# The tail of a two-layer decoder trunk: order of VectorE's scalings and last statistics, and low weight parts made by ScalarE and adding transfers

## The chip, the cores and the metric

The kernel runs on one core of a Trainium2 chip. The metric is the device time of one execution in microseconds; the median of three runs counts. A profile is one further execution, recorded by the hardware profiler, with a span from its first to its last instruction. The engines are TensorE (PE, its weight loads PEld), VectorE (DVE), ScalarE (ACT), GpSimd (POOL) and SyncE (SP), which issues nearly all DMAs.

## The reference

Two decoder layers over 256 positions of width 2048, all in float32. Layer 0 mixes by a gated short convolution, layer 1 by multi-head latent attention; each is followed by a squared-ReLU MLP of hidden width 8192, and every sub-layer ends in a layer norm of the scaled residual and the result. What matters here is the end:

```python
def sq_relu_mlp(x, w1, w2):
    return jnp.square(jax.nn.relu(x @ w1)) @ w2

h = layer_norm(ALPHA * h + mix, ln_g[layer, 0], ln_b[layer, 0])
h = layer_norm(ALPHA * h + sq_relu_mlp(h, mlp_w1[layer], mlp_w2[layer]),
               ln_g[layer, 1], ln_b[layer, 1])
```

## The kernel before, in words

**Two parts of a number.** TensorE multiplies in a rounded float32 form. To keep the precision, each operand is split in a high part (rounded) and a low part (what the rounding lost), and a product is the sum of three: high by high, high by low, low by high. A weight of 128 x 1024 numbers (a "half", 512 KB) is loaded into a buffer called raw (`load_raw`, issued on SP); `split` (L137 to L140) has ScalarE cast it into hi (L139) and VectorE subtract hi from raw into lo (L140). There are 7 raw buffers and 9 buffers of each part. A raw buffer comes free when its last reader, as a rule the subtraction on L140, is done.

**Slots.** An MLP (`mlp`) walks through a list of slots. A slot of the up-projection multiplies two w1 halves with the activations into ps_u (32 matmuls), which `evacuate` sums with a ScalarE copy (L401) and a VectorE addition (L402); beside it most slots multiply one "fast pair" of w2 weights, which go through a scheme of seven products in place of eight and need extra VectorE work: a difference of the two loads (L172), two more (L177, L179) and four splits, six steps in all (`prepare`, `to_step`). Each slot also prepares what the next one needs: its w1 halves (`singles`) and its pair (`pairs`). After each slot `order.keep()` ties the instructions of TensorE, VectorE and ScalarE to the order in which they were written. DMAs on SP and GpSimd are not tied; SP takes its own in one order, and a load waits there until a raw buffer is free. What comes after the slots is not tied on any engine: there the order is the one that the scheduler of the framework chose when the program was built.

**The end of the last MLP.** The last slots are (7, 7), with the last w1 halves and the third of four pairs, and (8, 0), with the last pair alone. Of w2's last quarter two column blocks are left over, n = 0 and n = 1, which are multiplied plainly: eight halves, called p0 to p7 here, p0 to p3 for n = 0 and p4 to p7 for n = 1. p0 to p4 are the singles of slot (8, 0); `take`, which looks ahead, prepares p5 to p7. `down_late` multiplies them for both token halves (t = 0: the first 128 positions, t = 1: the rest), t outside and n inside as written, so p0 serves twice. Between the first two blocks, `between` has VectorE finish the sums of the fast products (`fold_last`, L681) and take the statistics of the blocks 2 and 3.

**The last norm** (`to_out`). `finished` (L1204) takes statistics of each of the four blocks (L1205). After the last one of a token half, VectorE aggregates them (L1211) and computes the inverse deviation (rr, L431). For t = 0 it centres each block (L1219), scales it (L1222), and SP stores it (L1197). For t = 1, ScalarE makes diagonal matrices of means (L1232) and deviations (L1239), TensorE adds their products with gamma and beta (gbt) to three of the blocks (L1235) and one (L1240), VectorE scales three blocks (L1222) and ScalarE the last (L1244). The whole of gbt is loaded on SP (L1190), into the room that the activations of the up-projection leave.

**Adding transfers.** The first fold of the fast products (`fold`, g = 0, L668) is made by GpSimd DMAs which add one SBUF block to another.

Of the kernel before, what the change touches and what calls it, by code (L numbers as in the profile page):

```python
# [10 lines left out]
F32 = mybir.dt.float32  # L11
F32R = mybir.dt.float32r
AF = mybir.ActivationFunctionType
ALU = mybir.AluOpType
# [42 lines left out]
def trunk(ctx: ExitStack, tc: tile.TileContext, xT, vecs, lead, w_first, w_in, w_out, w_kv, w_q, w_uk, w_uv,  # L57
# [79 lines left out]
    def split(hi, lo, src):  # L137

        nc.scalar.copy(hi, src)  # L139
        return nc.vector.tensor_tensor(lo, src, hi.bitcast(F32), ALU.subtract)  # L140

    def tiled(w):
        return w.rearrange("p (b c) -> p b c", c=P)
# [9 lines left out]
    def prepare(i):  # L153

        if len(stream[i]) == 1:
            raw = loaded.pop(i) if i in loaded else load_raw(i, stream[i][0])
            hi, lo = ready[i] = parts(i)
            split(hi, lo, tiled(raw))
            yield
            return  # L160
        r1, r2 = (load_raw(f"{i}_{j}", src) for j, src in enumerate(stream[i]))
        t = raws.tile([P, 1024], F32, tag="raw", name=f"raw{i}_t")
        out = []

        def finished(r, name):
            hi, lo = parts(name)
            split(hi, lo, tiled(r))
            out.append((hi, lo))

        b22, (b21, b12) = r1[:, BW:], (r2[:, :BW], r2[:, BW:])  # L170
        two = "p (a c) -> p a c"
        nc.vector.tensor_tensor(t.rearrange(two, a=2), b12.unsqueeze(1).to_broadcast([P, 2, BW]),  # L172
                                r1.rearrange(two, a=2), ALU.subtract)
        yield
        finished(r1, f"{i}_1")
        yield
        nc.vector.tensor_tensor(b12, b22, t[:, :BW], ALU.subtract)  # L177
        t4 = r1[:, :BW]
        nc.vector.tensor_tensor(t4, b21, b12, ALU.subtract)  # L179
        yield  # L180
        finished(t, f"{i}_t")
        yield
        finished(r2, f"{i}_2")
        yield
        f = state["fast"].tile([P, 2, BW], F32R, tag="t4", name=f"t4_{i}", bufs=2)
        split(f[:, 0, :], f[:, 1, :], t4)
        b1, t13, b2 = ([[v.rearrange("p b c -> p (b c)")[:, o:o + BW] for v in w] for o in (0, BW)] for w in out)
        ready[i] = {"11": b1[0], "22": b1[1], "21": b2[0], "T2": b2[1], "T1": t13[0], "T3": t13[1],
                    "T4": [f[:, 0, :], f[:, 1, :]]}
        yield  # L190
# [2 lines left out]

        return 1 if len(stream[i]) == 1 else 6

    begun, loaded = {}, {}

    def step(i):

# [421 lines left out]
    def mlp(idx, ln, blocks, fast, begin=None, extra=None, last=False):  # L621
# [192 lines left out]
        for s, (q, m, pair, own) in enumerate(slots):  # L814
            lone = pair is None
            following = slots[s + 1][3] if s + 1 < len(slots) else []
            pairs = [i for i in following if size(i) > 1]
            far = slots[s + 2][3][-1:] if s + 2 < len(slots) and not pairs and lone else []
            far = [i for i in far if size(i) > 1]
            end = following[-1] + 1 if pairs else far[0] if far else own[-1] + 6  # L820
            singles = [i for i in range(state["next"], end) if i not in own and size(i) == 1 and i not in begun]
            for i in singles:
                loaded[i] = load_raw(i, stream[i][0])
            if q == FAST[0] and m == SHIFT:
                sums = act.tile([P, 4, 2, BW], F32, tag="xres", name=f"sums{idx}")
                for o, _, _ in FACTORS:
                    resume(o, 1)
            if q < NQ:
                w = take(2, 0)
                at = "6" if lone and (m - SHIFT) % 2 else "unit"  # L830
                un = psum("ps_u", bank[at])
                mm_run([(w, un)], xhl, 0, NC, NC, turned=TURNED if TURN(q, m) else None)

            def to_step(n):

                for i in pairs:
                    while i not in begun or begun[i][1] < n:
                        step(i)

            def evacuate():  # L840

                if q == NQ:
                    return
                if m % 2 == 0:
                    rows[m // 2] = fast.tile([P, 8 * P], F32, tag="fp", name="fp")
                u = rows[m // 2]
                whole(un, u[:, (m % 2) * T:(m % 2 + 1) * T])
                if m == QC - 1:
                    nc.vector.scalar_tensor_tensor(u[:, T:2 * T], u[:, T:2 * T], 0.0, u[:, T:2 * T], ALU.max, ALU.mult)
                    forms(u)  # L850
                    due.extend((m // 2, at) for at in columns(m))

            crowded = len(moves) > 0
            ends = q == NQ - 1 and m == QC - 1
            if q == NQ and last:
                last_sum(0, 0, bank["unit"])
            to_step(1)
            if not singles or m == 0 or q == NQ:
                split_due()
            for i in singles:  # L860
                step(i)
                move(1)
                drain()
                split_due()
            if crowded:
                evacuate()
                move(len(moves))
            if q == NQ - 1 and m == SHIFT and not last:
                fold_some(4)
            if q == NQ - 1 and m == 2:  # L870
                fold_some(8)
            if far:
                for i in far:
                    for _ in range(2):
                        step(i)
            if q == NQ - 1 and m == QC - 2 and not last:
                fold_some(4)
            hi_first = pairs and not crowded and q < NQ
            to_step(1 if hi_first else 2)
            if pair:  # L880
                products_of(*pair)
            if not crowded:
                if hi_first:
                    to_step(2)
                evacuate()
            move(1)
            to_step(3)
            if ends:
                split_due()
            to_step(4)  # L890
            move(1)
            to_step(5)
            move(1)
            to_step(6)
            move(1)
            if q < NQ:
                if m % 2 and m < QC - 1 or m == QC - 2:
                    u = rows[m // 2]
                    at = u[:, :T] if m == QC - 2 else u[:, :2 * T]
                    for function in (AF.Relu, AF.Square):  # L900
                        nc.scalar.activation(at, at, function)
                    if m % 2:
                        forms(u)
                    due.extend((m // 2, at) for at in columns(m))
                if extra and q == FAST[0] and m < NB:
                    for t in range(2):
                        extra(block, m, t, spare[1 + (2 * m + t) % 3])
                if begin and q == FAST[0] and m < 4 and m % 2 == 0:
                    nc.gpsimd.dma_start(parked[:, 4 * m:4 * m + 8, :], held_x[0][:, 4 * m:4 * m + 8, :])
                for i in far:  # L910
                    for _ in range(2):
                        step(i)
            order.keep()
# [273 lines left out]
    def to_out(block, finals, h, fold_last):  # L1187
# [8 lines left out]
        def store(t, i):  # L1196
            nc.sync.dma_start(out[t * P:(t + 1) * P, i * BW:(i + 1) * BW], block(i, t))  # L1197

        def scratch(i):
            return raws.tile([P, 1024], F32, tag="raw", name=f"u{i}")[:, :BW]  # L1200

        order = (2, 3, 0, 1)

        def finished(n, t, ps):  # L1204
            nc.vector.bn_stats(out=stats[:, t, n, :], in_=ps)  # L1205
            if n != order[-1]:
                if t == 1:
                    nc.vector.tensor_tensor(ps, ps, gbt[:, n, :BW], ALU.mult)
# [10 lines left out]
                nc.vector.scalar_tensor_tensor(us[i], finals[i, t], mv[:, 0:1], gbt[:, i, :BW], ALU.subtract, ALU.mult)  # L1219

            def scaled(i, x, other, op=ALU.add):
                nc.vector.scalar_tensor_tensor(block(i, t), x, r, other, ALU.mult, op)  # L1222
                store(t, i)

            if t == 0:
                rsqrt(r, ve)
                for i in order:
                    centred(i)
                    scaled(i, us[i], gbt[:, i, BW:])
                return  # L1230
            means = scratch("means")[:, :P]
            nc.scalar.activation(means, negative, AF.Copy, scale=mv[:, 0:1])  # L1232
            one = order[0]
# [4 lines left out]
            devs = scratch("devs")[:, :P]  # L1238
            nc.scalar.activation(devs, id_t, AF.Copy, scale=ve)  # L1239
            nc.tensor.matmul(finals[one, t], devs, gbt[:, one, BW:], start=False, stop=True, skip_group_check=True)  # L1240
            scaled(n, us[n], gbt[:, n, BW:])
            for i in order[1:-1]:
                scaled(i, finals[i, t], gbt[:, i, BW:])
            nc.scalar.activation(block(one, t), finals[one, t], AF.Copy, scale=r)  # L1244
            store(t, one)

# [105 lines left out]
```

## Time and profile before

| | |
|---|---|
| median of three runs | 1996.42 us (1995.43 to 1997.84) |
| profiled execution | 1996.9 us |
| its span | 1995.1 us |
| TensorE, VectorE, ScalarE, GpSimd busy | 99%, 88%, 64%, 1% |
| TensorE's mean granted clock | 0.998 |
| DMA moved | 394.19 MB, 198 GB/s on average |

A row of a timeline gives the start and the length in us, the engine, the line, the operation and what it writes and reads, and in brackets how long the engine was idle before and what ended that. Instructions of one kind in a row stand merged in one row (x5); they overlap at their edges, so that their sum of lengths is over their distance. A row of the windows gives, for each stretch, its length and the busy time and instructions of PE, PEld, DVE, ACT and POOL, then the granted clock of TensorE, the busy share of the DMA engines and GB/s. The chain of waits is followed back from the last instruction.

### The profile page before, as it was taken

What the parts mean: (1) busy time and instruction counts of PE and PEld (TensorE: products, weight loads), DVE (VectorE), ACT (ScalarE), POOL (GpSimd) and SP (SyncE); (2) the same over time, 40 slices, a digit from 0 to 9 for tenths busy, and PEclk for the clock granted to TensorE, in tenths of its full rate; (3) what the DMA queues carried; (4) which work ended last, traced back from release to release, by engine and by line L of the source; (5) the groups of instructions that cost most, each with busy time, mean ns of one, the idle gap of its engine ahead of it and who ended that gap; (6) DMA issues with size and microseconds to landing.
All of it is one profiled execution on the core that took longest, in us unless ns stands there. A gap on an engine that the chain in (4) does not pass through costs nothing.

```text
span 1995.1 us, 29544 instructions
## 1 busy us (share of the span) xinstructions
PE 1984.8 (99%) x11050; PEld 1730.0 (87%) x11050; DVE 1755.7 (88%) x2546; ACT 1278.5 (64%) x1872; POOL 19.7 (1%) x43
## 2 busy tenths in 40 slices
PE   9999999999999999999999999999999999999998
PEld 8888888988888888888889998898888888888886
DVE  8667667786999999999898988777899999999998
ACT  6444445585767767677656655557576776767763
POOL 0000000000000000000100000000000000000010
PEclk9999999999999999999999999999999999999999
DMA  9666666574566665566865544665366666666674
GB/s 342 212 190 188 190 190 190 178 236 131 200 203 203 210 202 192 206 204 211 270 245 159 181 137 131 187 191 180 127 211 201 201 197 203 211 203 202 198 231 158
DMA packets 110016, 394.19 MB, mean 198 GB/s; under 512 B 12208, under 2 KB 12976, under 8 KB 109360
## 3 DMA queue, kind: packets, MB, share of 16 engines
q1 hardware_dynamic: 106560, 383.79, 59.5%
q0 software_dynamic: 3168, 8.39, 1.7%
q8 instruction: 86, 1.41, 0.3%
q14 instruction: 58, 0.48, 0.1%
q10 hardware_dynamic: 144, 0.13, 0.0%
HBM read 383.87 MB, written 4.19 MB: 195 GB/s over the span
## 4 chain that ended last, share of the span: by engine, by line
PE 94%; DVE 3%; ACT 1%; DMA 1%; issue 1%; DVEq 0%; ACTq 0%
PE ps_u L256 20%; PE ps_l L256 13%; PE ps_u L260 10%; PE ps L343 7%; PE ps L344 7%; PE ps L341 7%; PE ps_l L260 7%; PE ps_d L344 2%; PE ps_d L343 2%; PE ps_d L341 2%; PE ps_w L290 1%; PE ps_w L288 1%; PE ps_w L289 1%; DVE lo L140 1%; PE ps_g L288 1%; PE ps_g L290 1%
## 5 line engine op out<-in xcount | busy, mean ns | idle before, releaser
L140 DVE TENSOR_TENSOR lo<-raw,hi 128x1024 fp32r<-128x1024 f32 x710 | 852.1, 1220 | 115.8 <-ACT hi L139 47.4
L139 ACT CAST hi<-raw 128x1024 fp32r<-128x1024 f32 x710 | 729.2, 1051 | 336.1 <-DVE raw L177 136.9
L256 PE MATMUL ps_u<-xhl,hi 128*128 128x512 f32 x1792 | 621.0, 393 | 0.4 <-DVE fp L402 0.3
L260 PE MATMUL ps_u<-xhl,lo 128*128 128x256 f32 x1792 | 485.4, 280 | 0.0
L256 PEld LDWEIGHTS ps_u<-xhl,hi 128*128 128x128 f32 x1792 | 329.1, 187 | 67.8 <-DVE fp L402 1.6
L260 PEld LDWEIGHTS ps_u<-xhl,lo 128*128 128x128 f32 x1792 | 338.0, 189 | 12.7
L256 PE MATMUL ps_l<-xhl_a,hi 128*128 128x512 f32 x704 | 244.1, 393 | 0.0
L260 PE MATMUL ps_l<-xhl_a,lo 128*128 128x256 f32 x704 | 195.4, 279 | 0.0
L256 PEld LDWEIGHTS ps_l<-xhl_a,hi 128*128 128x128 f32 x704 | 132.1, 188 | 29.9
L260 PEld LDWEIGHTS ps_l<-xhl_a,lo 128*128 128x128 f32 x704 | 131.9, 188 | 0.2
L172 DVE TENSOR_TENSOR raw_t<-raw,raw 128x1024 f32<-128x1024 f32 x100 | 121.8, 1218 | 1.6 <-DMA raw<-in_w2f_dram 1.6
L140 DVE TENSOR_TENSOR lo_t<-raw_t,hi_t 128x1024 fp32r<-128x1024 f32 x100 | 121.9, 1219 | 0.0
L401 ACT COPY t<-ps_u 128x256 f32<-128x256 f32 x112 | 41.5, 370 | 108.7 <-PE ps_u L260 108.4
L139 ACT CAST hi_t<-raw_t 128x1024 fp32r<-128x1024 f32 x100 | 105.3, 1053 | 0.1
L256 PE MATMUL ps_l<-z,hi 128*128 128x512 f32 x240 | 82.4, 391 | 0.0
L290 PE MATMUL ps_w<-xd,hi 128*128 128x258 f32 x256 | 72.7, 284 | 0.0
L288 PE MATMUL ps_w<-xd,hi 128*128 128x258 f32 x256 | 72.3, 282 | 0.0
L179 DVE TENSOR_TENSOR raw<-raw 128x512 f32<-128x512 f32 x100 | 69.2, 692 | 3.5
L289 PE MATMUL ps_w<-xd,lo 128*128 128x258 f32 x256 | 72.2, 282 | 0.0
L256 PE MATMUL ps_l<-oT,hi 128*128 128x512 f32 x208 | 71.3, 391 | 0.0
L402 DVE TENSOR_TENSOR fp<-ps_u,t 128x256 f32<-128x256 f32 x112 | 46.9, 418 | 27.7 <-ACT t L401 27.5
L140 DVE TENSOR_TENSOR t<-raw,t 128x512 fp32r<-128x512 f32 x100 | 68.5, 685 | 2.1 <-ACT t L139 1.6
(365 smaller groups left out, 3896.7 us busy)
## 6 DMA issues: line engine op xcount, KB each, us to landing
raw<-in_w_dram SPq DMA_DIRECT2D x312, 512.0 KB, 4.2
raw<-in_w2f_dram SPq DMA_DIRECT2D x200, 512.0 KB, 4.2
raw<-in_w_in_dram SPq DMA_DIRECT2D x88, 512.0 KB, 4.3
raw<-in_w_out_dram SPq DMA_DIRECT2D x32, 512.0 KB, 3.6
raw<-in_w_o_dram SPq DMA_DIRECT2D x32, 512.0 KB, 4.2
raw<-in_w_kv_dram SPq DMA_DIRECT2D x10, 512.0 KB, 5.0
raw<-in_w_q_dram SPq DMA_DIRECT2D x8, 512.0 KB, 4.0
raw<-in_w_uk_dram SPq DMA_DIRECT2D x8, 512.0 KB, 4.5
```

Source lines behind the costliest of these rows:

```text
L139: nc.scalar.copy(hi, src)
L140: return nc.vector.tensor_tensor(lo, src, hi.bitcast(F32), ALU.subtract)
L172: nc.vector.tensor_tensor(t.rearrange(two, a=2), b12.unsqueeze(1).to_broadcast([P, 2, BW]), r1.rearrange(two, a=2), ALU.subtract)
L179: nc.vector.tensor_tensor(t4, b21, b12, ALU.subtract)
L256: nc.tensor.matmul(ps, w[blk // 8][0][:, blk % 8, :], x, start=first, stop=False)
L260: nc.tensor.matmul(ps[:, :T], w[blk // 8][1][:, blk % 8, :], x[:, :T], start=False, stop=last)
L288: nc.tensor.matmul(ps[:, :W], hi, x[k][:, :W], start=k == 0, stop=False)
L289: nc.tensor.matmul(ps[:, :W], lo, x[k][:, :W], start=False, stop=False)
L290: nc.tensor.matmul(ps[:, :W], hi, x[k][:, W:], start=False, stop=k == NC - 1)
L341: nc.tensor.matmul(ps, x[0], w[0], start=first, stop=False, skip_group_check=onto)
L343: nc.tensor.matmul(ps[:, at], x[0], w[1][:, at], start=False, stop=False, skip_group_check=onto)
L344: nc.tensor.matmul(ps, x[1], w[0], start=False, stop=last, skip_group_check=onto)
```

## The change

It has two parts.

The first ties VectorE's order in the end. The last statistics (n = 1, t = 1) come behind the third scaling of t = 0. The fourth scaling of t = 0 (n = 1), with its store, is made only in the call for t = 1, behind the scaling of its block n, and the other two scalings of t = 1 follow in that order.

The second makes the low parts of p0 and p1 without VectorE. Both are loaded at the beginning of slot (7, 7), before the loads of the last pair. In that slot ScalarE casts hi, and then writes the negated hi into lo; a DMA of GpSimd adds the weight to it, which it reads from DRAM once more. p0's part stands ahead of `evacuate`, p1's behind it. In slot (8, 0) only p2 to p4 are left as singles.

```diff
@@ prepare
+            if i in summed_up:
+                nc.scalar.copy(hi, tiled(raw))
+                nc.scalar.activation(lo, hi.bitcast(F32), AF.Copy, scale=-1.0)
+                nc.gpsimd.dma_start(lo, tiled(stream[i][0]), accum_op=ALU.add)
+            else:
+                split(hi, lo, tiled(raw))
@@ mlp, the loop over slots
-            for i in singles:
+            ends = q == NQ - 1 and m == QC - 1
+            plain = [slots[-1][3][-1] + 1 + i for i in range(2)] if ends and last else []
+            summed_up.update(plain)
+            for i in singles + plain:
                 loaded[i] = load_raw(i, stream[i][0])
...
+                for i in plain[:1]:
+                    step(i)
                 evacuate()
+                for i in plain[1:]:
+                    step(i)
@@ to_out
+        def after(made, other):
+            tc.add_manual_dep(made.ins, other.ins.name, mybir.DependencyInfo(
+                mybir.DependencyClass.NoSync, mybir.DependencyReason.DATA), reason="order")
+            return made
...
-            nc.vector.bn_stats(out=stats[:, t, n, :], in_=ps)
+            made = nc.vector.bn_stats(out=stats[:, t, n, :], in_=ps)
+            if n == order[-1] and t:
+                after(made, later[0])
...
                 for i in order:
                     centred(i)
-                    scaled(i, us[i], gbt[:, i, BW:])
+                    if i != order[-1]:
+                        made = scaled(i, us[i], gbt[:, i, BW:])
+                later.extend((made, lambda: scaled(order[-1], us[order[-1]], gbt[:, order[-1], BW:])))
...
-            scaled(n, us[n], gbt[:, n, BW:])
+            made = scaled(n, us[n], gbt[:, n, BW:])
+            made = after(later[1](), made)
             for i in order[1:-1]:
-                scaled(i, finals[i, t], gbt[:, i, BW:])
+                made = after(scaled(i, finals[i, t], gbt[:, i, BW:]), made)
```

More of the change, by code (lines that the diff above doesn't have):

```diff
@@ L157, in prepare @@
             hi, lo = ready[i] = parts(i)
-            split(hi, lo, tiled(raw))
+            if i in summed_up:
[4 more added lines that the diff above has]
+                split(hi, lo, tiled(raw))
             yield
@@ L194, in size @@
         return 1 if len(stream[i]) == 1 else 6
-    begun, loaded = {}, {}
+    begun, loaded, summed_up = {}, {}, set()
     def step(i):
@@ L853, in mlp @@
             crowded = len(moves) > 0
-            ends = q == NQ - 1 and m == QC - 1
             if q == NQ and last:
@@ L1200, in scratch @@
             return raws.tile([P, 1024], F32, tag="raw", name=f"u{i}")[:, :BW]
-        order = (2, 3, 0, 1)
+        order, later = (2, 3, 0, 1), []
+        def after(made, other):
+            tc.add_manual_dep(made.ins, other.ins.name, mybir.DependencyInfo(
+                mybir.DependencyClass.NoSync, mybir.DependencyReason.DATA), reason="order")
+            return made
         def finished(n, t, ps):
-            nc.vector.bn_stats(out=stats[:, t, n, :], in_=ps)
+            made = nc.vector.bn_stats(out=stats[:, t, n, :], in_=ps)
+            if n == order[-1] and t:
+                after(made, later[0])
             if n != order[-1]:
@@ L1221, in scaled @@
             def scaled(i, x, other, op=ALU.add):
-                nc.vector.scalar_tensor_tensor(block(i, t), x, r, other, ALU.mult, op)
+                made = nc.vector.scalar_tensor_tensor(block(i, t), x, r, other, ALU.mult, op)
                 store(t, i)
+                return made
             if t == 0:
```

## The prediction

> **What bounds the kernel now.** I read the page first, then the timeline of the last 50 us engine by engine, then the clock in windows of 1 us.
>
> ```profile
> span 1995.1 us, 29544 instructions
> PE 1984.8 (99%) x11050; PEld 1730.0 (87%) x11050; DVE 1755.7 (88%) x2546; ACT 1278.5 (64%) x1872; POOL 19.7 (1%) x43
> ```
>
> TensorE is busy for 99% of the span, so only its few idle spells can be won, and nearly all of them lie in the last 50 us, where the change is. The profiled execution took 1996.9 us, 1.8 more than its span; the median of the runs is 1996.42, 0.5 below it. I work out a difference against the span and subtract it from the median.
>
> ```profile
> 1958.02 0.39 PE L341 MATMUL ps_e<-hi,h3c 128*128 128x512 f32 x1
> 1958.24 0.39 PE L343 MATMUL ps_e<-lo,h3c 128*128 128x512 f32 x1
> ...
> 1964.82 0.39 PE L341 MATMUL ps_e<-hi,h3c 128*128 128x512 f32 x1
> 1965.71 0.50 PE L341 MATMUL ps_e<-hi,h3c 128*128 128x512 f32 x1 [0.51 <-ACT hi L139]
> ...
> 1980.35 0.39 PE L344 MATMUL ps_e<-hi,h3a 128*128 128x512 f32 x1
> ```
>
> The two plain blocks start at 1958.02. They are 96 matmuls (2 token halves, 2 blocks, 8 tiles of the hidden dimension, 3 matmuls each). Thirty steps lead from 1958.02 to 1964.82, 0.2267 us each. Unhindered, the last would start 95 steps on, at 1979.56, and end at 1979.95; it ends at 1980.74. The 0.79 us are the wait at 1965.71 for the high part of p5, whose load was late.
>
> ```profile
> 1956.29 5.76 DVE L140 TENSOR_TENSOR lo<-raw,hi 128x1024 fp32r<-128x1024 f32 x5
> ...
> 1963.78 0.68 DVE L1205 BATCH_NORM_STATS2 stats<-ps_e 128x6 f32<-128x512 f32 x1
> ...
> 1965.69 1.23 DVE L140 TENSOR_TENSOR lo<-raw,hi 128x1024 fp32r<-128x1024 f32 x1 [0.64 <-ACT hi L139]
> ...
> 1979.94 0.15 DVE L431 SCALAR_TENSOR_TENSOR rr<-ra,rt 128x1 f32<-128x1 f32 x1
> 1980.78 0.70 DVE L1205 BATCH_NORM_STATS2 stats<-ps_e 128x6 f32<-128x512 f32 x1 [0.69 <-PE ps_e L344]
> 1981.39 2.72 DVE L1222 SCALAR_TENSOR_TENSOR acc<-u,rr,gbt 128x512 f32<-128x512 f32 x4
> 1984.03 0.26 DVE L1211 BATCH_NORM_AGGREGATE mv<-stats 128x2 f32<-128x24 f32 x1
> ...
> 1986.14 0.75 DVE L1222 SCALAR_TENSOR_TENSOR acc<-u,rr,gbt 128x512 f32<-128x512 f32 x1 [0.28 <-DVE rr L431]
> 1988.66 0.75 DVE L1222 SCALAR_TENSOR_TENSOR acc<-ps,rr,gbt 128x512 f32<-128x512 f32 x1 [1.76 <-PE ps L1235]
> ```
>
> VectorE sets what comes next. It is busy from 1956.29 to 1980.09 except for 0.64 us. The last statistics run at 1980.78, as soon as TensorE ends. Then the four scalings of the first token half stand for 2.72 us between these statistics and the aggregation at 1984.03, though nobody waits for them.
>
> ```profile
> 1984.84 3.78 PE L1235 MATMUL ps<-gbt,umeans 128*128 128x512 f32 x4 [4.10 <-ACT umeans L1232]
> ...
> 1988.41 1.68 PE L1235 MATMUL ps_e<-gbt,umeans 128*128 128x512 f32 x2
> ...
> 1989.92 1.02 PE L1240 MATMUL ps<-gbt,udevs 128*128 128x512 f32 x2
> ```
>
> TensorE resumes at 1984.84, 0.81 us after the aggregation starts, for eight passes over the means and deviations. They end at about 1990.94, 0.04 before ScalarE's last scaling:
>
> ```profile
> 1955.03 4.85 ACT L139 CAST hi<-raw 128x1024 fp32r<-128x1024 f32 x5
> ...
> 1990.98 0.69 ACT L1244 ACTIVATE acc<-ps,rr 128x512 f32<-128x512 f32 x1 [4.30 <-PE ps L1240]
> ```
>
> ```profile
> 1982.00:1983.00 1.00, 0.00 (x0) 0.00 (x0) 1.00 (x3) 0.00 (x0) 0.00 (x0) 0.95 0.00 0
> 1983.00:1984.00 1.00, 0.00 (x0) 0.00 (x0) 1.00 (x2) 0.00 (x0) 0.00 (x0) 0.50 0.98 381
> ...
> 1989.00:1990.00 1.00, 1.00 (x3) 0.41 (x2) 0.41 (x1) 0.00 (x0) 0.00 (x0) 0.64 0.00 0
> ...
> 1993.00:1994.00 1.00, 0.00 (x0) 0.00 (x0) 0.00 (x0) 0.00 (x0) 0.00 (x0) 0.57 0.23 88
> ```
>
> The granted clock (the value after TensorE's, VectorE's, ScalarE's and GpSimd's columns) falls to half at 1982.9, 2.2 us after the matmuls end, and is back at about 1989.7. It falls again at 1993.14, 2.2 us after the last pass. So most of the eight passes ran at half speed.
>
> **The order, alone.** Three scalings go before the last statistics, and the fourth behind a scaling of the second half. If VectorE were no earlier than now, they would start 0.28 us after 1980.09 (the wait behind rr in the row of 1986.14), take 3 x 0.66 plus 0.06 us, end at 1982.41 less the 0.06 of overlap, and 0.61 us later (1980.78 to 1981.39) the aggregation would start at 1982.96: **1.07 us** sooner. The fourth scaling, 0.66 us, fits into the 1.76 us for which VectorE waits before 1988.66, and costs nothing; without that cover it would delay two scalings and their stores by 0.66. Its store moves with it on SP, 0.33 us of issue as in SP's rows below, ahead of stores that are later anyway.
>
> **The subtractions.** p0 and p1 no longer need VectorE: five subtractions (5.76 us, 1.14 apart) become three, **2.28 us** less. With the 0.64 us of waiting for p5 gone, rr can be ready at 1977.2 and the three scalings done at 1979.5, ahead of TensorE. Then TensorE's end E is the bound: statistics 0.04 later, aggregation 0.61 after that, passes 0.81 later: **E + 1.46**. With E at 1979.95 that is 1981.41 instead of 1984.84, **3.43 us** sooner, the 1.07 included. What is late next is E itself.
>
> **ScalarE.** For p0 it makes a cast and a negated copy between these rows, for p1 the same after the copy of ps_u:
>
> ```profile
> 1945.55 1.04 ACT L139 CAST hi<-raw 128x1024 fp32r<-128x1024 f32 x1
> 1948.57 0.37 ACT L401 COPY t<-ps_u 128x256 f32<-128x256 f32 x1 [1.98 <-PE ps_u L260]
> 1951.12 1.06 ACT L139 CAST h3a<-fp 128x1024 fp32r<-128x1024 f32 x1 [2.18 <-DVE fp L700]
> ```
>
> A cast costs 0.95 us in a row of casts (4.85 for five, less the last 1.05). The negated copy of this shape is not in the trace; its bounds are nothing beyond a cast's 0.95 and, generously, twice it; I take 1.05, as it reads and writes what the cast does. From 1946.50 p0's two end at 1948.5, in the idle 1.98 us; p1's run from 1948.94 to 1950.9, in the idle 2.18. Both are hidden, by 0.1 to 0.2 us. Queued behind p0's is the copy of ps_u, for which VectorE waits; at twice the price VectorE would lose 0.9 of its 2.28 us.
>
> **Loads.** p0 and p1 are now asked for ahead of the last pair's two loads and take the buffers that were theirs:
>
> ```profile
> 1935.09 0.93 SPq L150 DMA_DIRECT2D raw<-in_w2f_dram  x2
> ...
> 1941.22 0.33 SPq L150 DMA_DIRECT2D raw<-in_w_dram  x1
> ...
> 1954.66 0.33 SPq L150 DMA_DIRECT2D raw<-in_w_dram  x1
> ...
> 1956.04 1.82 SPq L150 DMA_DIRECT2D raw<-in_w_dram  x3
> ```
>
> p0 and p1 load at 1935.09 and 1935.69, the pair at about 1938.9 and 1941.22, when the buffers of two w1 halves come free. The pair is read here:
>
> ```profile
> 1946.78 1.22 DVE L172 TENSOR_TENSOR raw_t<-raw,raw 128x1024 f32<-128x1024 f32 x1
> ```
>
> That leaves 5.6 us for a landing; nothing to pay. SP goes in order, so p0 and p1 hold up only the pair. Their buffers come free when ScalarE has read them, so p4 loads at 1947.6 instead of 1954.66 and p5 at about 1950 instead of 1956.04. In the chain of waits p5 took this long:
>
> ```profile
> 1956.04 8.55 DMA raw<-in_w_dram
> ```
>
> At six microseconds of head start, p5 can stand the adding transfers' traffic ahead of it, and the wait of 0.79 us goes. I count it as gone; kept, it costs that much.
>
> **The adding transfers** carry the risk. GpSimd reads p0 from DRAM again and adds it to the negated high part. It has nothing else to do after its last such transfer:
>
> ```profile
> 1910.67 0.86 POOL L668 DMA_DIRECT2D acc<-sums  x1 [4.24 <-DVE fp L402]
> 1915.57 0.87 POOL L668 DMA_DIRECT2D acc<-sums  x1 [4.04 <-issue]
> 1920.82 0.87 POOL L668 DMA_DIRECT2D acc<-sums  x1 [4.38 <-issue]
> 1927.62 0.88 POOL L668 DMA_DIRECT2D acc<-sums  x1 [5.93 <-issue]
> ```
>
> These four add 256 KB each within SBUF. They don't all depend on one another, yet each starts 4.9 to 6.8 us after the one before, though issuing takes 0.87: with "issue" as releaser, GpSimd waited for nothing that the profile shows. The landing times of all sixteen are
>
> ```profile
> DMA to landing us min/median/max: 3.2/5.8/8.7
> ```
>
> so I read this as one adding transfer at a time, each when the last has landed. Plain 512 KB transfers by GpSimd land after
>
> ```profile
> DMA to landing us min/median/max: 5.2/6.6/7.9
> ```
>
> An adding 512 KB transfer from DRAM is not in the trace. Its bounds are 3.2 and 8.7 us; I take 6.5, near the plain one of its size. The first is issued at 1948.56 and lands at 1955.1. TensorE wants it at 1958.24, so 3.1 us of cover. The second then starts, and not when its ScalarE part is ready at 1950.9: it lands at 1961.7 (with 0.1 for the start). TensorE wants p1's low part seven steps after 1958.02, at 1959.6. **It waits S = 2.1 us**, at every matmul behind it too, as its queue goes in order. By the bounds S is 0 (landing at 1955.0) to 6.4 (1966.0); p0 is in time at both.
>
> By the Trainium skill, page "DMA: Bandwidth & Descriptors", section "Anatomy of one DMA — SWDGE (gpsimd) path", a transfer of GpSimd takes about 2.0 us and its bytes over 436 GB/s; an estimate from that is 3.2 us for 512 KB, and S would be 0. The median landing of 5.8 us at half the size does not agree.
>
> **The clock in the end.** TensorE's gap before the passes shrinks from 4.10 to 1.46 us. Twice the clock fell 2.2 us after the last matmul, so I let it hold. Eight passes took 6.1 us, six of them 0.855 apart; all at full clock would take 3.45: **2.65 us** less. VectorE's and ScalarE's remaining steps follow the passes. The bounds are 0 and 2.65.
>
> The Trainium skill, page "TensorE: Matmul & The Clock Gate", section "What's actually happening", has the clock judged in free-running windows of 3413 ns. The times 1982.9, 1989.7 and 1993.14 agree: two windows and one. By that rule a gap of 1.46 us is at most 43% of a window, and the two windows that ended in a fall were 63% idle; where between them the limit lies no run shows.
>
> **Sum.** -3.43 + 2.1 - 2.65 = **-4.0 us**: 1992.9 for the profiled execution, **1992.4** on the median.
>
> **Rivals.**
> Transfers in time: two of 3.2 us one after the other, or two that don't wait for each other. S is 0: -6.1, so 1990.3. For it: the lightly loaded rows reach 3.2. Against: loads for p2 to p5 and the norm's factors share the DMA engines just then. The page on DMA speaks for this one.
> VectorE not relieved: if it keeps to its order and waits for TensorE's first plain block (the statistics of ps_e at 1963.78 follow that block by 0.2 us), its 2.28 us are lost there. Only the order's 1.07 is won; the gap before the passes is then 3.8 us and the clock falls as now: 1995.3. This is also the case in which the relief doesn't do what it says.
> Transfers late, the slower side: at 8.7 us each, S is 6.4, and during such an idle the clock falls, so that after it 3.4 to 6.8 us (the second from the rows of 1983 to 1989.7, the first its half) run at half speed, losing 1.7 to 3.4, say 2.6. -3.43 + 6.4 + 2.6 = +5.6, 2002.0; with the gain of 2.65 in the end, +2.9, 1999.3. It decides from where S and the lost clock exceed 6.1 us: the second landing after 1965.7, or after 1963.1 if the clock falls.
>
> **How the numbers follow.** Forecast 0.42, in time 0.25, not relieved 0.16, late 0.17. The forecast's own range is 1990.5 to 1995.5 (S from 1 to 4, the clock held or not). The whole range is 1990.0 to 2000.0: the best case at 1990.3 and most of the late one; left out are the rest of the late case (0.1) and a little below. 0.2% is 4.0 us, about what a measurement of this kernel can tell from no change: the bound is 1992.4, in the middle of the forecast. Faster: half of 0.42, and 0.18 of the 0.25 (where the clock falls it is -3.4): 0.39. Slower: 0.11 of the late case and 0.02 of mishaps: 0.13. Within: 0.48.
>
> **What would show it.** GpSimd's second adding transfer starting about 6 us after the first; a wait of TensorE on a DMA at p1's first low part, and its length; no wait before p5; the three scalings ahead of the last statistics, the aggregation 0.65 us after TensorE's end; a gap before the passes of about 1.5 us and passes 0.43 apart. I am wrong if TensorE's order in the plain blocks changes so that p1's low part is used later, if VectorE ends after TensorE, or if the clock falls in either gap.

## The result and the profile after

The kernel after took 2002.17 us (median of 10 runs, 1999.84 to 2003.54) against 1995.93 for the kernel before (10 runs, 1994.86 to 1999.73), a ratio of 1.0028 with a 95% interval of 1.0018 to 1.0038: slower by 0.28%, 6 us. The forecast was 1992.4, the range ended at 2000.0. The sum of the rival "transfers late" (2002.0) is what came.

The profiled execution took 2002.73 us, 5.8 more than that of before. Its page begins

```profile
span 2001.0 us, 29547 instructions
...
PE 1984.4 (99%) x11050; PEld 1729.7 (86%) x11050; DVE 1753.7 (88%) x2544; ACT 1277.9 (64%) x1874; POOL 21.5 (1%) x45
```

TensorE does the same work in the same busy time. The span is 5.9 us longer, so TensorE is idle for longer. The added lines shift the numbers: the plain blocks' matmuls are now on L346, L348 and L349, the statistics on L1221, the passes on L1257 and L1262, the scalings on L1240, ScalarE's two new steps on L159 and L160, the adding transfers on L161. TensorE's timeline, where the bracket gives the idle time before and what ended it:

```profile
1958.54 0.39 PE L346 MATMUL ps_e<-hi,h3c 128*128 128x512 f32 x1
1960.04 0.50 PE L348 MATMUL ps_e<-lo,h3c 128*128 128x512 f32 x1 [1.11 <-DMA lo<-in_w_dram]
...
1969.02 0.79 PE L348 MATMUL ps_e<-lo,h3c 128*128 128x512 f32 x1 [7.33 <-DMA lo<-in_w_dram]
...
1990.52 0.39 PE L349 MATMUL ps_e<-hi,h3a 128*128 128x512 f32 x1
1992.49 1.98 PE L1257 MATMUL ps<-gbt,umeans 128*128 128x512 f32 x4 [1.58 <-ACT umeans L1254]
1994.31 1.02 PE L1257 MATMUL ps_e<-gbt,umeans 128*128 128x512 f32 x2
1995.17 1.02 PE L1262 MATMUL ps<-gbt,udevs 128*128 128x512 f32 x2
```

TensorE waits for both adding transfers: 1.11 us for p0's low part at its first use, and 7.33 us for p1's. The gap before the passes is 1.58 us where it was 4.10, and the passes are 0.43 apart. GpSimd's timeline and SP's say why the waits are so long:

```profile
1949.53 0.88 POOL L161 DMA_DIRECT2D lo<-in_w_dram  x1 [20.76 <-PE ps_u L265]
1960.31 0.88 POOL L161 DMA_DIRECT2D lo<-in_w_dram  x1 [9.90 <-ACT sums L664]
```

```profile
1946.79 1.59 SPq L150 DMA_DIRECT2D raw<-in_w_dram  x3
1949.17 1.82 SPq L1201 DMA_DIRECT2D gbt<-in_gb_dram  x4
1951.09 5.58 SPq L150 DMA_DIRECT2D raw<-in_w_dram  x3
```

By the trace's landing records the first transfer lands at 1960.00, 10.47 us after its issue; the second is issued 0.31 us later and lands at 1968.97, 8.67 us after. ScalarE had finished p1's part at 1951.59 (1950.53 + 1.06), so the second transfer was ready for 8.7 us before GpSimd issued it. SP has meanwhile issued three weights and all four of gbt's loads in a run. In the chain of waits the last 50 us hang on these transfers:

```profile
1950.41 9.88 issue
...
1960.31 8.67 DMA lo<-in_w_dram
...
1969.02 0.79 PE ps_e L348
```

"issue" for 9.88 us is GpSimd waiting for nothing that the profile shows, which is how the fold's transfers looked in the profile before. During the long wait the clock falls. Windows of 2 us (the last three values are granted clock, DMA share and GB/s):

```profile
1955.00:1957.00 2.00, 2.00 (x11) 1.60 (x10) 2.00 (x4) 2.00 (x4) 0.00 (x0) 1.00 1.05 297
...
1962.00:1964.00 2.00, 0.00 (x0) 0.00 (x0) 1.32 (x3) 0.00 (x0) 0.00 (x0) 1.00 1.02 416
1964.00:1966.00 2.00, 0.00 (x0) 0.00 (x0) 0.20 (x1) 1.04 (x1) 0.00 (x0) 0.80 1.11 317
1966.00:1968.00 2.00, 0.00 (x0) 0.00 (x0) 1.03 (x1) 0.88 (x1) 0.00 (x0) 0.50 0.88 205
...
1970.00:1972.00 2.00, 2.00 (x6) 1.57 (x5) 0.00 (x0) 0.79 (x1) 0.00 (x0) 0.50 0.00 0
```

The DMA engines are full (share 1.0) from 1955 to 1966. Where only plain loads run (1962 to 1964) they move 416 GB/s, and 297 to 317 where an adding transfer runs beside them. Where TensorE resumes at 1969.02 it runs at half clock until about 1972.

VectorE's end went as forecast:

```profile
1985.75 0.69 DVE L1221 BATCH_NORM_STATS2 stats<-ps_e 128x6 f32<-128x512 f32 x1
1986.36 2.06 DVE L1240 SCALAR_TENSOR_TENSOR acc<-u,rr,gbt 128x512 f32<-128x512 f32 x3
...
1990.94 0.70 DVE L1221 BATCH_NORM_STATS2 stats<-ps_e 128x6 f32<-128x512 f32 x1 [1.92 <-PE ps_e L349]
1991.68 0.26 DVE L1229 BATCH_NORM_AGGREGATE mv<-stats 128x2 f32<-128x24 f32 x1
```

The three scalings stand ahead of the last statistics, VectorE then waits for TensorE, and the aggregation starts 0.77 us after TensorE's end (1990.91).

**Where 5.9 us come from.** Unhindered, the plain blocks would take 21.93 us from their start (95 steps of 0.2267 and the last matmul's 0.39). Before they took 22.72, 0.79 more; now they take 32.37 (1958.54 to 1990.91), 10.44 more. So 9.65 us are lost there. Of the 10.44, the two waits are 8.44. The half clock costs 1.51: the seven steps from 1969.02 to the matmul at 1972.12 take 3.10 us, and 7 x 0.2267 is 1.59. Most of the other 0.49 goes with starting again: a bracket counts from the end of the matmul before, 0.16 later than a step does, and the first step after the first wait takes 0.34. The tail wins 2.52 in the gap (4.10 to 1.58) and 2.40 in the eight passes (6.10 to 3.70). The plain blocks start 0.52 later; in the profiles of the experiments they start between 1956.95 and 1959.49, so this probably belongs to the single execution. From the end of ScalarE's last scaling to the span's end it takes 4.0 us and not 3.4, 0.6 more: the last five stores now follow each other 0.63 to 0.67 us apart, and the last lands 2.93 us after its issue instead of 2.35. In the experiments that last landing takes 2.56 to 2.95 us where the stores stand as close, and 2.35 to 2.39 where they don't. 9.65 - 2.52 - 2.40 + 0.52 + 0.6 is 5.85, so nearly nothing is left over.

### The profile page after: what moved, and what is told of

The parts are those of the page before. It is cut to its first block, busy times and chain, and to the rows that moved or that the text cites. A ratio compares the mean times of both kernels' runs of the same rounds, so it can differ in the third digit from the quotient of the medians.

```text
span 2001.0 us, 29547 instructions
## 1 busy us (share of the span) xinstructions
PE 1984.4 (99%) x11050; PEld 1729.7 (86%) x11050; DVE 1753.7 (88%) x2544; ACT 1277.9 (64%) x1874; POOL 21.5 (1%) x45
## 4 chain that ended last, share of the span: by engine, by line
PE 95%; DVE 2%; issue 2%; DMA 1%; ACT 1%; POOL 0%; DVEq 0%; POOLq 0%; ACTq 0%
PE ps_u L261 20%; PE ps_l L261 13%; PE ps_u L265 10%; PE ps L348 7%; PE ps L349 7%; PE ps L346 7%; PE ps_l L265 7%; PE ps_d L349 2%; PE ps_d L348 2%; PE ps_d L346 2%; PE ps_w L295 1%; PE ps_w L293 1%; PE ps_w L294 1%; PE ps_g L293 1%; PE ps_g L295 1%
```

## The experiments

**Theory.** The adding transfers are the whole loss: each lands 8 to 12 us after its issue, since the DMA engines are full of loads that were issued before it, and the second isn't issued before the first has landed. Order and relief win what was worked out. **Rivals:** the tie costs by itself, ScalarE's and GpSimd's work hurts whatever the landings are, or gbt's place alone is the cause.

**The order alone.** The list of halves for the adding transfers is empty.

```diff
-            plain = [slots[-1][3][-1] + 1 + i for i in range(2)] if ends and last else []
+            plain = [slots[-1][3][-1] + 1 + i for i in range(0)] if ends and last else []
```

> The changed kernel with an empty list of plain halves: only the order is tied. Theory (the adding transfers alone cost time, the tie gains): 1 to 3.5 us faster than before, as the aggregation of the second token half starts 1.07 us sooner or more and the gap before the passes is shorter than 4.1 us. Rival (the tie itself costs, because the last statistics now wait for three scalings): 0 to 2 us slower than before.

1994.09 us against 1996.14 for before, ratio 0.9988 (0.9979 to 0.9997). TensorE's end in it:

```profile
1979.84 0.39 PE L349 MATMUL ps_e<-hi,h3a 128*128 128x512 f32 x1
1983.12 3.68 PE L1257 MATMUL ps<-gbt,umeans 128*128 128x512 f32 x4 [2.90 <-ACT umeans L1254]
```

The gap is 2.90 us for 4.10, so the order wins 1.20 there (1.07 forecast). The clock still falls: four passes take 3.68 us. The loss is not the tie's.

**The transfers alone.** The ties are taken out, the four scalings stand together as before.

> The changed kernel without the tied order: only the two adding transfers. Theory: two waits of TensorE on them of about 1.1 and 7.3 us as in the changed kernel, a half-speed spell, and four scalings ahead of the last aggregation: 7 to 10 us slower than before. Rival (the tie costs): less slow than the changed kernel, that is below 5 us.

2000.05, ratio 1.0019 (1.001 to 1.0028). That is 2.1 us less than the kernel after, and the expectation that the loss would be greater without the tie has failed. The tie costs only a small part of these 2.1 us, though. GpSimd's timeline:

```profile
1947.00 0.88 POOL L161 DMA_DIRECT2D lo<-in_w_dram  x1 [23.97 <-ACT lo L160]
1955.92 0.88 POOL L161 DMA_DIRECT2D lo<-in_w_dram  x1 [8.04 <-ACT hi L139]
```

Here the first transfer is issued 0.69 us ahead of gbt's first load (1947.69), and not 0.36 behind it; it lands at 1955.61, in time. The edit touches only the last norm, so what changes the order at this place isn't shown. TensorE waits once, 6.3 us, instead of 8.44 in two waits, but the clock is then at half until 1970.31: the plain blocks take 30.94 us, 1.4 less than in the kernel after. And the tie has nothing to win here, since the waiting TensorE leaves VectorE ahead: all four scalings are done at 1986.2, the last matmul ends at 1988.01, and the gap is 1.6 us without any tie. Behind ScalarE's last scaling the span ends after 3.5 us, and in the kernel after after 4.0, with its closer stores: in that half microsecond the rival is right. The tie's gain exists only where VectorE is late.

**Room for descriptors.** The kernel reserves 512 for the descriptors of GpSimd's transfers; here it is 576.

```diff
-dynamic_dma_scratch_size=512
+dynamic_dma_scratch_size=576
```

> The changed kernel with 576 in place of 512 bytes for GpSimd's DMA descriptors. Theory (the second adding transfer waits for room for its descriptors): it starts at about 1951.7, within 2.5 us of the first, instead of 10.8 us after it; both then share the DMA engines, the second lands 3 to 5 us sooner, TensorE's second wait falls from 7.3 to 2 to 4 us, and the time is 3 to 6 us below that of the changed kernel. Rival (adding transfers are kept apart whatever the room): it starts 0.3 us after the first has landed, as before, and the time stays within 1 us.

1998.74, ratio 1.0011 (1.0002 to 1.0021), 3.4 us less than after.

```profile
1949.94 0.88 POOL L161 DMA_DIRECT2D lo<-in_w_dram  x1 [41.06 <-ACT lo L160]
1952.92 0.86 POOL L161 DMA_DIRECT2D lo<-in_w_dram  x1 [2.10 <-ACT lo L160]
```

The second transfer is issued 2.98 us after the first, as soon as ScalarE's part is done, and not when the first has landed (1960.56). So the wait that the profile calls "issue" was for this room: changing the room alone removed it. The fold's transfers, too, go two at a time then: two are issued at 1900.75 and 1902.59, and the third 0.31 us after the first has landed. The two that the change adds are now under way together and take 10.62 and 12.02 us; TensorE waits 3.4 us in two waits, and the clock still falls behind them.

**gbt later.** The four loads of gbt are written behind the fold's last step, so that SP can take weights first.

```diff
-        for n in range(NB):
-            nc.sync.dma_start(gbt[:, n, :], gb[n].partition_broadcast(P))
...
+            for n in range(NB):
+                nc.sync.dma_start(gbt[:, n, :], gb[n].partition_broadcast(P))
```

> The changed kernel with the four loads of gamma and beta asked for behind the loads of the plain halves. Theory (an adding transfer waits behind the loads issued before it): the first lands after 7 to 8 us instead of 10.5, TensorE's first wait is gone, the second falls from 7.3 to 3 to 5 us, the time is 3 to 6 us below that of the changed kernel. Rival (an adding transfer of 512 KB from DRAM takes 9 to 10 us whatever lies before it): landings and waits stay within 1 us of the changed kernel's.

1999.75, ratio 1.0018 (1.0009 to 1.0027), 2.4 less than after, where 3 to 6 was expected. The first transfer lands 7.98 us after its issue instead of 10.47 and is in time; the second still takes 9.38 and costs 6.3 us. Two of the four loads went ahead of p6 and p7 all the same.

**Both remedies.** 576, and gbt later.

> The kernel after with both remedies at once: 576 in place of 512 for the descriptors of GpSimd's transfers, and gbt's four loads behind the fold's last step in the program. Theory (the size of the landings has two causes that add up: no room for a second transfer's descriptors, and loads that stand ahead in the DMA engines): the first transfer lands at about 1955.5, the second is issued 3 us behind the first and lands at 1959.5 to 1962; TensorE waits 0 to 2.5 us for p1's low part and not for p0's; clock full between 1958 and 1978 or nearly so; 1991.5 to 1995.5. Rival (the two remedies take away the same delay): no better than the larger room alone, 1998 to 2000.

1994.62, ratio 0.9995 (0.9986 to 1.0004).

TensorE's only wait among the plain blocks is

```profile
1961.17 0.50 PE L348 MATMUL ps_e<-lo,h3c 128*128 128x512 f32 x1 [0.93 <-DMA lo<-in_w_dram]
```

The transfers are issued at 1948.93 and 1951.93 and land after 7.45 and 9.20 us, and no fall of the clock follows. 7.5 of the 8.44 us are gone: the two causes together make up nearly all of the waits. Taken away alone, they were worth 5.0 us of waits (the room) and 2.1 (gbt's place).

**Plain transfers in their place.** The addition is left out, so that the low parts of p0 and p1 hold the weight itself; bytes, place and order stay.

```diff
-                nc.gpsimd.dma_start(lo, tiled(stream[i][0]), accum_op=ALU.add)
+                nc.gpsimd.dma_start(lo, tiled(stream[i][0]))
```

> The two adding transfers become plain ones of the same bytes from the same place; the addition of the negated high part is left out, so that the low parts of p0 and p1 hold the weight itself. Theory (an adding transfer needs more room for descriptors and takes about twice as long for a packet): the second is issued under 4 us after the first and does not wait for its landing; both land by 1961.5; TensorE waits 3 us or less in all; about 1992 to 1996. Rival (what delays them is the loads that stand ahead in the DMA engines, whatever the kind of transfer): the first lands at about 1960 and the second not before 1965 all the same; TensorE waits over 4 us; 1997 or more.

One execution took 1991.39 us, beside 1996.2 for before.

```profile
1947.41 0.57 POOL L161 DMA_DIRECT2D lo<-in_w_dram  x1 [19.78 <-ACT lo L160]
1950.53 0.56 POOL L161 DMA_DIRECT2D lo<-in_w_dram  x1 [2.54 <-ACT lo L160]
```

With 512 of room the second plain transfer is issued 3.12 us after the first; they land after 6.88 and 7.63 us, and TensorE waits for neither. The gap before the passes is 1.65 us. This is the forecast's kernel with S = 0, and it gives the time of the rival "transfers in time" (1990.3) within 1.1 us. The DMA view from 1945 to 1972 of the kernel after and then of this one (packets, MB, share of 16 engines) shows the price of adding:

```profile
q0 software_dynamic: 288, 1.05, 19.5%
```

```profile
q0 software_dynamic: 288, 1.05, 10.7%
```

The packets of the same 1.05 MB take 5.3 us of all 16 engines (19.5% of 27) when they add and 2.9 us when they don't; a packet of 4 KB takes 0.33 and 0.17 us (medians).

**One half.** p0 by ScalarE and an adding transfer, p1 by VectorE.

```diff
+            plain = [slots[-1][3][-1] + 1 + i for i in range(1)] if ends and last else []
```

> Only p0's low part is made by ScalarE and an adding transfer; p1 goes the old way again, VectorE's order stays tied. Theory (the second transfer, 10.8 us behind the first, costs the wait of 7.3 us and the spell at half clock; each transfer by itself costs little): one adding transfer, issued about 1949.5 and landed about 1960; TensorE waits at p0's low part by 0 to 1.5 us and nowhere else by more than 1; the clock doesn't fall between 1958 and 1978; 8 to 11 us faster than the kernel after, so 1991 to 1994.5. Rival A (any adding transfer there disturbs loads and VectorE as much as two): still above 1998. Rival B (the time lost is proportional to the transfers): half way between the kernel with the order alone (1994.1) and the kernel after (2002.2), about 1998.

1993.59, ratio 0.9988 (0.9979 to 0.9997), as expected. The transfer is issued at 1949.00 and lands 9.67 us later, TensorE waits for it nowhere, and the clock stays at 1.00 from 1958 to 1974. The second transfer is what makes the kernel after slow.

**The last two halves.** p6 and p7 instead of p0 and p1; their loads still stand ahead of the last pair's.

```diff
+            plain = [slots[-1][3][-1] + 7 + i for i in range(2)] if ends and last else []
```

> The two halves that ScalarE and the adding transfers make are p6 and p7, the last ones, instead of p0 and p1; their loads and ScalarE steps stay where p0's and p1's were. TensorE wants their low parts some 14 us later, at about 1971 and 1973. Theory (the landing of 8 to 12 us each, one at a time, is too long for the place of use, and nothing else is wrong with the transfers): the transfers are issued and landed as in the kernel after, at about 1960 and 1969; TensorE doesn't wait for them; VectorE is relieved of two subtractions and TensorE ends at 1980 to 1981; gap ahead of the passes 1.5 us, full clock there; 1990 to 1993.5. Rival (VectorE's relief is worth nothing, or the early halves' loads, now five behind the pair, come late behind the transfers): TensorE waits for high or low parts of p0 to p5 by over 2 us in all; 1995 or more.

1996.48, ratio 1.0003 (0.9994 to 1.0012): the expectation of the theory has failed, that of the rival holds. The transfers land at 1955.55 and 1965.10, and TensorE doesn't wait for them. It waits for something else. ScalarE's and TensorE's timelines:

```profile
1961.83 1.05 ACT L139 CAST hi<-raw 128x1024 fp32r<-128x1024 f32 x1 [4.03 <-DMA raw<-in_w_dram]
1962.78 2.04 ACT L664 COPY sums<-ps 128x512 f32<-128x512 f32 x4
1964.69 1.66 ACT L693 COPY ps_e<-acc 128x512 f32<-128x512 f32 x3
```

```profile
1965.37 0.79 PE L346 MATMUL ps_e<-hi,h3c 128*128 128x512 f32 x1 [2.81 <-ACT ps_e L693]
```

p4's load is issued only at 1953.60, behind two of gbt's loads, and lands 8.15 us later. ScalarE, in order, holds the copies behind p4's cast, and TensorE waits 2.81 us for the first of those on L693; the clock falls there too.

**The last two halves, gbt later.**

> As the kernel with p6 and p7, and gbt's four loads stand behind the fold's last step in the program, so that SP can take them after loads of the plain halves. Theory (gbt's loads, ahead in the DMA engines, delay transfers and loads; with 14 us of room nothing waits for them any more): the same as the kernel with p6 and p7 within 1 us. Rival (the loads of p3 to p5 are late there behind gbt): 1 to 3 us faster than that kernel, with fewer waits of TensorE and VectorE on DMAs.

1992.96, ratio 0.9986 (0.9977 to 0.9995), 3.5 us less than without gbt's move: the rival is right, and its 1 to 3 us were too few. p4's cast waits 1.66 us for its load instead of 4.03. TensorE's timeline:

```profile
1963.23 0.50 PE L346 MATMUL ps_e<-hi,h3c 128*128 128x512 f32 x1 [0.45 <-ACT ps_e L693]
1965.24 0.74 PE L346 MATMUL ps_e<-hi,h3c 128*128 128x512 f32 x2 [0.35 <-ACT hi L139]
...
1982.06 1.98 PE L1255 MATMUL ps<-gbt,umeans 128*128 128x512 f32 x4 [1.52 <-ACT umeans L1252]
```

TensorE waits 0.8 us, the gap is 1.52, and the clock holds. It is the fastest kernel here with the reference's output.

**Its control.** The order, gbt later, no adding transfers.

> The order tied and gbt's loads later, no adding transfers: all low parts by VectorE. It is the control for the kernel with p6 and p7 and gbt later (1993.0). Theory (that kernel's gain comes half from the order and half from VectorE's relief, and gbt's place matters only beside the transfers): as the order alone, 1993 to 1995, with a gap ahead of the passes of 2.5 to 3 us as there. Rival (gbt's place is itself the gain, since p5's load no longer comes late): the same as the kernel with p6 and p7, 1992.5 to 1993.3, with the gap under 2 us.

1993.71, ratio 0.9989 (0.998 to 0.9998), with this gap:

```profile
1983.16 1.98 PE L1255 MATMUL ps<-gbt,umeans 128*128 128x512 f32 x4 [2.93 <-ACT umeans L1252]
```

So gbt's place adds nothing that can be told from the order alone (1994.09). VectorE's relief shows in the profiles, as 2.93 us of gap against 1.52, but 1992.96 and 1993.71 are not told apart by the runs: the intervals overlap. Of the 3.2 us that the fastest kernel wins on before, the tied order alone wins 2.05.

## Why the prediction was wrong

**The step that failed** is the size of the adding transfers' landing: "its bounds are 3.2 and 8.7 us; I take 6.5". They took 10.47, beyond the upper bound, and 8.67, and the second couldn't start before the first had landed. With that, TensorE waited not S = 2.1 us but 8.44 in two waits, and p0's "3.1 us of cover" was gone. The bounds came from rows of the fold, 256 KB each, in a stretch where the DMA engines were less full (a share of 0.86 from 1898 to 1932 in the kernel before, against 1.0 to 1.1 from 1955 to 1966 here), and from plain transfers of GpSimd. Three things were missing. The engines were full: the experiment with gbt later cut the first landing by 2.5 us, and the plain transfers at the same place still took 6.88 and 7.63 against a median of 6.6. Adding costs 1.8 times the engine time of a plain copy. And the bytes of the whole stretch were never added up: six weights, four of gbt's loads and two adding transfers are 6.3 MB, which at the 416 GB/s of the plain stretch take 15.1 us, and some 2.4 more for the adding. The DMA view has the first bytes of this stretch at about 1948, so that even engines that never stand idle are full until 1965.5; the last weight landed at 1969.66.

**How it came about** lies in a part that the prediction had right and didn't follow to its end. It said that p0's and p1's buffers come free early, so that p4 loads at 1947.6 instead of 1954.66. It did, at 1948.05 (the third load of the row of 1946.79). But in the kernel before, SP stood at that load, and half of gbt's loads stood behind it until 1955.04:

```profile
1948.56 0.80 SPq L1190 DMA_DIRECT2D gbt<-in_gb_dram  x2
1954.66 0.33 SPq L150 DMA_DIRECT2D raw<-in_w_dram  x1
1955.04 0.91 SPq L1190 DMA_DIRECT2D gbt<-in_gb_dram  x2
```

With the buffers free, p4 and all of gbt went out by 1950.99, 1.5 MB earlier than before and right around the first adding transfer. The prediction named this sharing as an argument against a rival and gave it no price.

**One transfer at a time** was right: the second started 0.31 us after the first landed (0.1 forecast). The room for descriptors is the cause, as the change to 576 shows.

**Order** was right in the gap: 1.20 us for 1.07. What it put at nothing was the fourth scaling's store, which now stands among the last ones: the end is 0.6 us longer in the kernel after, and no longer with the order alone. **Subtractions** were right: "E + 1.46" became E + 1.65 with plain transfers, where TensorE waits for nothing in the plain blocks, and E + 1.52 with the last two halves and gbt later, where it waits 0.8 us. The E + 1.58 of the kernel after is no test, since its waiting TensorE leaves VectorE ahead anyway. With the order alone the gap was 2.90, so the relief is worth 1.25 to 1.4 us of gap. The forecast's 2.36 for it were 0.79 of p5's wait and 1.57 of gap (3.03 to 1.46). p5's wait did go with one half and with the plain transfers.

**ScalarE** was right: the negated copy takes 1.06 us (1.05 taken). p0's part ended at 1949.12 and the copy of ps_u started at 1949.17, so its cover was used to the last in this execution.

```profile
1946.98 1.05 ACT L159 CAST hi<-raw 128x1024 fp32r<-128x1024 f32 x1
1948.06 1.06 ACT L160 ACTIVATE lo<-hi 128x1024 fp32r<-128x1024 f32 x1
1949.17 0.37 ACT L406 COPY t<-ps_u 128x256 f32<-128x256 f32 x1
```

**Loads** were wrong for p5: issued at 1951.09 (about 1950 forecast), it landed at 1964.71, 13.6 us later, though six microseconds of head start were to be enough. It cost nothing only because TensorE was waiting for p1.

**The clock in the end** was right: it held through 1.58 us, and the passes won 2.40 of the 2.65. What the forecast lacked is the fall within the wait, 1.51 us; the rival had 2.6 for it.

**The rival's sum** was met with other terms. "Transfers late" had +5.6 from S = 6.4 and 2.6 of lost clock without the gain in the end. The run had 8.44 and 1.51, and the end's 2.40 as a gain. Its landings were worse than its own bound (19.1 us together for 17.4), and the tail was better than it allowed: two errors that cancel. Its point of decision, a second landing after 1963.1 to 1965.7, was passed by 3 us.

What stays open is why the first data of GpSimd's transfers move so late in this stretch (below).

## What to carry to other kernels

Before a transfer is put where the DMA engines are busy, add up all bytes that are issued in that stretch, with adding transfers at nearly twice their size, and divide by the rate of the busiest window; the landing times of a quieter stretch are no bound. A buffer that comes free earlier lets the issuing queue run ahead, and what stood behind it in that queue comes out all at once: list those transfers too. Two adding transfers of GpSimd may have to wait for each other, which a gap put down to "issue" gives away, so a second one needs its landing counted from the first one's.

## What the runs showed of the hardware

A GpSimd transfer of 512 KB landed 6.88 to 12.02 us after its issue in this stretch, plain or adding. The Trainium skill, page "DMA: Bandwidth & Descriptors", section "Anatomy of one DMA — SWDGE (gpsimd) path", has about 2.0 us and the bytes over 436 GB/s, by which an estimate is 3.2 us; no run here came near it. By the trace's packet records the first data of the first transfer moved 5.8 us after its issue in the kernel after, against 1.8 to 3.2 us for the last four of the fold's. Over the experiments this time goes with the place among gbt's loads: it is 2.9 to 3.2 us in the six profiles in which the transfer was issued 0.28 us or more ahead of gbt's first load, 4.3 and 4.9 us where it was 0.23 and 0.16 us ahead, and 5.8 us in the kernel after, where it was 0.36 us behind. Why so little makes so much isn't shown.

Whether a gap makes the clock fall is not settled by its length. With the order alone, after a gap of 2.90 us, four passes took 3.68 us, at half speed; with gbt later, after 2.93 us, the same four took 1.98. The granted clock in the two, order alone first:

```profile
1983.00:1984.00 1.00, 0.88 (x1) 0.44 (x2) 0.83 (x5) 0.17 (x2) 0.00 (x0) 0.61 0.37 113
1984.00:1986.00 2.00, 2.00 (x4) 0.89 (x3) 1.56 (x3) 0.69 (x2) 0.00 (x0) 0.50 0.11 43
```

```profile
1983.00:1984.00 1.00, 0.84 (x2) 0.49 (x3) 0.85 (x4) 0.20 (x2) 0.00 (x0) 1.00 0.42 127
1984.00:1986.00 2.00, 2.00 (x6) 0.92 (x5) 1.94 (x4) 0.70 (x2) 0.00 (x0) 1.00 0.09 35
```

Both gaps began at 1980.23 of their spans. The Trainium skill, page "TensorE: Matmul & The Clock Gate", section "What's actually happening", has activity judged in windows of 3413 ns that run free of the kernel; the two gaps, equal in length and place and different in outcome, agree. Gaps of 1.52 to 1.69 us held in all eight kernels that had one, and one of 2.57 us held with one half.

The traces show what decides. By their clock records the granted clock changes only at edges that lie whole numbers of 3.413 us apart. With the order alone one edge is at 1983.22; in the 3.413 us ahead of it 2.89 us are gap, so that this stretch is 85% idle, and the clock falls. With gbt later the edges, counted back from the fall at 1988.93, are at 1982.10 and 1985.52, and the gap is shared by two stretches that are 55% and 31% idle. Laid over all twelve profiles, no such stretch at full clock that was up to 55% idle by the matmuls' rows ended in a fall, and each that was 58% idle or more did. Once at half clock, stretches 47% to 57% idle did not bring it back, and those up to 11% idle did. So the prediction's open limit, between 43% and 63%, lies between 55% and 58% here, and whether such a gap costs the clock depends on where an execution's edges fall. An estimate from these shares: a gap under 1.9 us (55% of 3.413), with no other idle time around it, does no harm, one over 4.0 us (twice 58%) always does, and between them it may.
